# Moving the row tiles 2 to 4 of an output projection from their own stage into the last steps of a scan

## The chip, the cores and the metric

One core of a Trainium2 chip runs the whole program. The metric is device time in microseconds (us) for one execution, lower is better.

## The reference

One layer of a diffusion backbone over 2048 latent tokens of width 1024, with 256 context tokens. What matters here is the middle: a projection gives the inputs of three groups of heads (pooling, Mamba-2 SSD, gated DeltaNet), whose outputs stand beside each other as the 1024 columns of the mixer's output, and one output projection follows with a gated residual; then a router and a mixture of experts.

```python
s_lat, _, _ = ssd_stream(pl[1], pl[2], pl[3], *ssd_p, ssd_sf, ssd_sb)
g_lat, _, _ = gdn_stream(to_column_major(pl[4]), ...)          # a scan over chunks of 64, both directions
lat = jnp.concatenate([pool_branch(pl[0], pool_w, pool_scale), s_lat, g_lat], axis=-1) @ w_out
...
x = x + m_lat[2][:, None] * mix_lat
h_lat = modulate(rms_norm(x, norm2_g[l]), m_lat[3], m_lat[4])
x = x + m_lat[5][:, None] * expert_choice_ffn(h_lat, router_w[l], ...)
```

Of the 1024 rows of `w_out` (8 row tiles of 128) the tiles 0 and 1 meet the pooling's columns, 2 to 4 the SSD's and 5 to 7 the DeltaNet's.

## The kernel before, in words

The program has four stages: the input projection (to some 760 us), the scan (some 800 to 1523 us), the output stage (projection, norm and router, to 1713 us) and the mixture of experts.

**The scan** is recorded step by step from a list `plan`: `at(when, f)` puts a piece of work at a place `when`, counted in steps, and the pieces are recorded sorted by it. There are 36 chunk steps of the DeltaNet (`NSTEP`); preparing a chunk (`gdn_prep`, `gdn_inv`) runs ten steps (`LAG`) ahead of the chain `gdn_chain(n)`, which carries the state from chunk to chunk and so stands at the places n + 9.9 to n + 10.7. The SSD (`ssd_f`) stands at the places 9 to 28. From place 36 on only the chain and its last merges are left: the drain. TensorE's instructions keep the recorded order while the scan is recorded (`TE.order`, which ties each to the one before); on the other engines, and after the scan on TensorE too, a scheduler orders them.

A step of the chain: `pv<-kv` and `pv<-gS,w` (matmuls into the bank `pv`), ACT copies `vn` out of it; `po<-gS,qg` and `po<-vn,xqr` make the output in the bank `po`, of which there is one; `pc<-vn,ke` and DVE's `gS` make the next state. In its second half a step also adds the other direction (`po<-oe,turned`), and `gdn_out` scales the result out of `po` (ACT `osq`, a few small DVE operations, DVE `oe`) and stores it (`go_d<-oe`). The `pm` matmuls belong to `gdn_w` and to the merges of the triangular inverse.

**The fills.** The mixer's outputs of pooling and SSD lie in `mix_d`, transposed, before the DeltaNet is done. A fill multiplies some row tiles of one token tile t (16 of them) into one column half c (2 of 512), adds a partial sum and stores it: in `x0_d`, from which the output stage goes on. `sums[c][t]` holds how many row tiles are done and where the sum lies. `fill` is a generator in three pieces: the loads (`mx` from `mix_d`, `x`, which is the tile `fx`), the split of `mx` in a high and a low part (ACT and DVE), and the multiplication, `mm3` per row tile (three matmuls, high by high, high by low, low by high), with the DVE add and the store. Before the change the fills do row tiles 0 and 1 (`K0 = 2`), one per step: the first column half at the places 4 to 19, the second at 20 to 35, six matmuls each, in the bank `po`. The tile `fx` has three buffers, the `mx` tile (`fm`) and its parts (`fmh`, `fml`) two.

**The output stage.** `prep(t)` loads the row tiles that are left (`mx`), the chain's output `go` (four DMAs) and the partial sums `xo`; it splits row tiles 2 to 4, transposes `go` on TensorE, multiplies it into the last three row tiles (the gate) and splits them. `project(t)` multiplies the row tiles from `sums[h][t][0]` to 8 for both halves. `router(t)` transposes the new rows, multiplies them by the router's weights and writes the normed rows `h2`.

The weights of row tiles 2 to 4 are loaded by `load_1` (first half, place 36.5) and `ssd_end` (second half, place 28.5, when the SSD's tiles come free).

## Time and profile before

| | us |
|---|---|
| median of 3 timed runs | 2447.54 (2445.14 to 2454.45) |
| the profiled execution | 2454.28 |
| its span in the trace | 2452.5 |
| TensorE busy | 2119.1 (86%) |
| DVE, ACT, POOL busy | 1512.6, 1010.9, 771.3 |
| mean granted TensorE clock | 0.914 |

The busy time of an engine is an average over stages that have different limits, and a matmul's listed duration overlaps the next one's. So the stretches around the change are read one by one. PE is TensorE's multiplications, PEld its weight loads, DVE is VectorE, ACT ScalarE, POOL GpSimd, SP SyncE. A clock of 1.00 is 2.4 GHz all the time, 0.50 would be 1.2 GHz all the time.

### The profile page before, as it was taken

The page shows a single profiled execution, that of the slowest core. Times are in us where ns is not written, and L with a number is a line of the kernel's source. Part 1 is how long each engine was busy: PE and PEld are TensorE (multiplying, and loading weights), DVE is VectorE, ACT ScalarE, POOL GpSimd, SP SyncE. Part 2 cuts the span into 40 slices and gives each one's busy share as a digit, 9 for nine tenths or more (in the row PEclk, how much of TensorE's full clock was granted, in tenths as well). Part 3 has the DMA queues.
Part 4 walks back from the last instruction along what each step waited for, and adds up shares of the span by engine and source line. Part 5 has one row for each costly group of instructions (what it writes and reads, how often), then busy time and mean ns, then how long its engine had stood idle before and what let it go on. Part 6 is the DMA issues. An engine that isn't in the chain of part 4 may idle for free. (4 is left out here: it accounts for less than half of the span.)

```text
span 2452.5 us, 55979 instructions
## 1 busy us (share of the span) xinstructions
PE 2119.1 (86%) x22825; PEld 1816.0 (74%) x22825; DVE 1512.6 (62%) x3357; ACT 1010.9 (41%) x1916; POOL 771.3 (31%) x712
## 2 busy tenths in 40 slices
PE   4789999989987688989878788999199999988886
PEld 2788888878865467768766676787199999987785
DVE  6766776756755544545535443544757667689876
ACT  5443334544324235434443222454144444455552
POOL 1002332354421524434422122344331111124453
PEclk8899999999988779989998778999599999999998
DMA  7442345665435956666655432754447787778883
GB/s 233 117 110 91 82 124 145 168 172 126 128 86 143 277 146 167 166 175 184 186 163 154 138 94 73 244 197 139 171 156 212 233 227 223 231 256 282 303 283 138
DMA packets 323452, 425.77 MB, mean 174 GB/s; under 512 B 48875, under 2 KB 214650, under 8 KB 322170
## 3 DMA queue, kind: packets, MB, share of 16 engines
q1 hardware_dynamic: 294266, 356.07, 48.8%
q0 software_dynamic: 14816, 50.03, 7.7%
q10 hardware_dynamic: 14112, 16.10, 1.9%
q8 instruction: 179, 2.93, 0.5%
q14 instruction: 79, 0.65, 0.1%
HBM read 302.80 MB, written 126.71 MB: 175 GB/s over the span
## 5 line engine op out<-in xcount | busy, mean ns | idle before, releaser
L90 PE MATMUL pj<-hTh,wh 128*128 128x512 f32 (+1 forms) x800 | 308.6, 386 | 4.7 <-ACT wh L221 3.8
L90 PE MATMUL pj<-hTl,wh 128*128 128x512 f32 (+1 forms) x800 | 309.0, 386 | 0.0
L90 PE MATMUL pj<-hTh,wl 128*128 128x512 f32 (+1 forms) x800 | 307.8, 385 | 0.9 <-DVE wl L222 0.9
L491 DVE SCALAR_TENSOR_TENSOR acc<-u,PV,acc 128x512 f32<-128x512 f32 (+1 forms) x320 | 273.1, 900 | 55.0 <-ACT acc L489 36.4
L1727 ACT ACTIVATE wh<-wr 128x1024 fp32r<-128x1024 f32 x192 | 202.3, 1056 | 252.5 <-PE pgate L90 74.6
L1729 DVE TENSOR_TENSOR wl<-wr,wh 128x1024 fp32r<-128x1024 f32 x176 | 223.7, 1276 | 102.4 <-ACT wh L1727 102.2
L90 PEld LDWEIGHTS pj<-hTh,wh 128*128 128x128 f32 x800 | 154.2, 193 | 36.8 <-ACT wh L221 4.1
L90 PEld LDWEIGHTS pj<-hTh,wl 128*128 128x128 f32 x800 | 153.6, 192 | 31.7 <-DVE wl L222 1.6
L90 PEld LDWEIGHTS pj<-hTl,wh 128*128 128x128 f32 x800 | 154.0, 192 | 30.2 <-issue 0.7
L90 PE MATMUL pgate<-xel,wh 128*128 128x256 f32 x512 | 150.6, 294 | 2.9 <-DVE xel L222 2.9
L90 PE MATMUL pgate<-xeh,wh 128*128 128x256 f32 x512 | 148.7, 290 | 3.8 <-ACT xeh L221 3.7
L90 PE MATMUL pgate<-xeh,wl 128*128 128x256 f32 x512 | 150.1, 293 | 0.0
L90 PE MATMUL pup<-xeh,wh 128*128 128x256 f32 x512 | 149.1, 291 | 0.0
L90 PE MATMUL pup<-xel,wh 128*128 128x256 f32 x512 | 147.5, 288 | 0.0
L90 PE MATMUL pup<-xeh,wl 128*128 128x256 f32 x512 | 147.5, 288 | 0.0
L542 POOL TENSOR_TENSOR aw<-aw,sc 128x1024 f32<-128x1024 f32 x32 | 66.1, 2065 | 256.5 <-DMA aw<-in_ada_w_dram 252.0
L1826 POOL DMA_INDIRECT x_d<-ye,idx x30 | 48.8, 1626 | 203.2 <-DVE ye L1820 128.6
L90 PE MATMUL pdown<-wh,hh 128*128 128x512 f32 x256 | 103.3, 403 | 7.4 <-DVE ye L1820 3.0
L1128 ACT ACTIVATE Db<-xk 32x192 f32<-32x192 f32 (+2 forms) x160 | 55.1, 344 | 126.1 <-DVE xk L1111 124.6
L90 PEld LDWEIGHTS pgate<-xeh,wh 128*128 128x128 f32 x512 | 101.1, 198 | 5.1 <-ACT xeh L221 4.8
L90 PEld LDWEIGHTS pgate<-xel,wh 128*128 128x128 f32 x512 | 101.1, 198 | 3.1 <-DVE xel L222 3.1
L90 PE MATMUL pdown<-wh,hl 128*128 128x512 f32 x256 | 100.6, 394 | 0.6 <-DVE hl L222 0.6
(562 smaller groups left out, 5520.6 us busy)
## 6 DMA issues: line engine op xcount, KB each, us to landing
wr<-in_exp_w_gate_dram SPq DMA_DIRECT2D x64, 512.0 KB
wr<-in_exp_w_up_dram SPq DMA_DIRECT2D x64, 512.0 KB
wr<-in_exp_w_down_dram SPq DMA_DIRECT2D x64, 512.0 KB
aw<-in_ada_w_dram SPq DMA_DIRECT2D x32, 512.0 KB
kq<-qk_d SPq DMA_DIRECT2D x36, 384.0 KB
xb<-xb_d SPq DMA_DIRECT2D x35, 320.0 KB
wr<-in_w_in_dram SPq DMA_DIRECT2D x21, 512.0 KB
aw<-in_ada_w_dram SPq DMA_DIRECT2D x8, 1024.0 KB
```

Of the source, the lines that this page charges most:

```text
L90: return self.pin(nc.tensor.matmul(*args, **kw))
L491: V.scalar_tensor_tensor(av, u[:, s0 - 2 + i:s0 - 2 + i + w], cw[:, i, cb:cb + 1], av, op0=OP.mult, op1=OP.add)
L542: G.tensor_tensor(w, w, sc2[:, :, 0:1].to_broadcast([P, KT, P]), op=OP.mult)
L1128: S.activation(D_b[b][QS[q], sl:sl + w, :], xk[QS[q], h0:h0 + w, c:c + 32], AF.Copy)
L1727: S.activation(wh, w, AF.Copy)
L1729: (G if nw[0] <= 16 else V).tensor_tensor(wl, w, wh.bitcast(F32), op=OP.subtract)
L1826: G.indirect_dma_start(out=x2_d, out_offset=rows_of(e, h), in_=ys[h], in_offset=None, compute_op=OP.bypass if late else OP.add)
```

## The change

The fills are of three kinds now. `fill_0` is as before, for the first column half alone (places 4 to 19). `fill_1` takes the second column half, row tiles 0 to 4 in one go (15 matmuls), at the places 31 to 45.25, 0.95 apart. `fill_2` takes the first half again, row tiles 2 to 4 (9 matmuls), from `x0_d` to the new `x1_d`, at the places 38.4 to 45.9, half a step apart. Both use the ring `pp` of three banks in place of `po`, and tiles `fk`, `fkh`, `fkl` (two buffers each) in the room that the SSD leaves. `load_0(1)` moves from place 20 to `ssd_end`. Since `prep` and `project` go by `sums`, the output stage has row tiles 5 to 7 left, 18 matmuls per token tile where there were 36.

```diff
--- before.py
+++ after.py
@@ -185,6 +185,7 @@
     mrow_d = dram("mrow_d", [4, D])
     mcol_d = dram("mcol_d", [P, 16])
     x0_d = dram("x0_d", [T, D])
+    x1_d = dram("x1_d", [T, D])
     x2_d = dram("x2_d", [T, D])
     h2_d = dram("h2_d", [T, D])
 
@@ -1297,7 +1298,7 @@
             V.tensor_tensor(wl, w, wh.bitcast(F32), op=OP.subtract)
         wo[c].update(rows)
 
-    def fill(c, t, k1, dst, tiles):
+    def fill(c, t, k1, dst, tiles, ring):
 
         k0, src = sums[c][t]
         sums[c][t] = k1, dst
@@ -1309,19 +1310,36 @@
         yield
         split(mh, ml, mx)
         yield
-        po = bank(pb, "po", [512], 1)
+        po = bank(pb, ring, [512], NPP if ring == "pp" else 1)
         for k in range(n):
             mm3(po, mh[:, k, :], ml[:, k, :], *wo[c][k0 + k], k == 0, k == n - 1)
         V.tensor_tensor(x, po, x, op=OP.add)
         SY.dma_start(dap(dst, t * P * D + 512 * c, [[D, P], [1, 512]]), x)
 
-    def fill_0(c, t):
-        if t == 0:
+    def late_tiles(n):
+        return [wps[0].tile([P, KA, P], F32R if q else F32, name="fk" + q, bufs=2)[:, 0:n] for q in ("", "h", "l")]
+
+    def load_0(c):
+        if True:
             wh, wl = (p0.tile([P, K0, 512], F32R, name="f" + q) for q in "hl")
             load_wout(c, {k: (wh[:, k, :], wl[:, k, :]) for k in range(K0)},
                       (p0.tile([P, 512], F32, name="fx", bufs=3) for _ in range(3)))
-        return fill(c, t, K0, x0_d, lambda n: [p0.tile([P, K0, P], F32R if q else F32, name="fm" + q, bufs=2)
-                                               for q in ("", "h", "l")])
+
+    def fill_0(t):
+        if t == 0:
+            load_0(0)
+        return fill(0, t, K0, x0_d, lambda n: [p0.tile([P, K0, P], F32R if q else F32, name="fm" + q, bufs=2)
+                                               for q in ("", "h", "l")], "po")
+
+    def fill_1(t):
+
+        return fill(1, t, KA, x0_d, late_tiles, "pp")
+
+    def fill_2(t):
+
+        return fill(0, t, KA, x1_d, late_tiles, "pp")
+
+    wps = []
 
     def rows_3(tiles):
         return {K0 + k: tuple(t[:, k * 512:(k + 1) * 512] for t in tiles) for k in range(KA - K0)}
@@ -1377,15 +1395,22 @@
     for t in range(18):
         j = SSD0 + t
         along(ssd_f(t), *(j + q for q in (-0.4, 0.12, 0.26, 0.46, 0.56, 0.64, 0.74, 1.05, 1.9)))
-    for i, (c, t) in enumerate((c, t) for c in range(2) for t in range(NT)):
-        gen = []
-        at(FILL0 + i - 0.9, lambda c=c, t=t, gen=gen: gen.append(fill_0(c, t)) or next(gen[0]))
-        for q in (-0.3, 0.04):
-            at(FILL0 + i + q, lambda gen=gen: next(gen[0], None))
+    def fills(f, place):
+        for t in range(NT):
+            gen = []
+            at(place(t) - 0.9, lambda t=t, gen=gen: gen.append(f(t)) or next(gen[0]))
+            for q in (-0.3, 0.04):
+                at(place(t) + q, lambda gen=gen: next(gen[0], None))
+
+    fills(fill_0, lambda t: FILL0 + t)
+    fills(fill_1, lambda t: SSD0 + 22 + 0.95 * t)
+    fills(fill_2, lambda t: NSTEP + 2.4 + 0.5 * t)
 
     def ssd_end():
         stS.close()
         wp = stS.enter_context(tc.tile_pool(name="wout", bufs=1, reuse_waits="tile"))
+        wps.append(wp)
+        load_0(1)
         load_wout(1, rows_3([wp.tile([P, (KA - K0) * 512], F32R, name="wo" + q) for q in "hl"]),
                   (wp.tile([P, 512], F32, name="wr", bufs=4) for _ in range(4)))
 
```

What this does to TensorE's order, at one step of the drain. Before, from the output matmuls of a chain step to the state's part of the next one (`pm<-y` and `pm<-Yt` are the merge's and `gdn_w`'s; each row stands for all that follow each other, so x12 is a row of small matmuls):

```order
L90 MATMUL po<-vn,xqr 64x64 x12
L90 MATMUL po<-oe_16610,turned 128x384
L90 MATMUL pm<-y_16763,A_6362 64x32 x12
L90 MATMUL pv<-kv,Yt_6368 64x64 x12
L90 MATMUL pm<-Yt_6369,kw 64x64 x12
L90 MATMUL pv<-gS,w 64x64 x12
```

And in the changed kernel:

```order
L90 MATMUL po<-vn,xqr 64x64 x12
L90 MATMUL po<-oe_16679,turned 128x384
L90 MATMUL pm<-y_16854,A_6363 64x32 x12
L90 MATMUL pv<-kv,Yt_6369 64x64 x12
L90 MATMUL pm<-Yt_6370,kw 64x64 x12
L90 MATMUL pp<-kq,fkh 128x512 x2
L90 MATMUL pp<-kq,fkl 128x512
L90 MATMUL pp<-kq,fkh 128x512 x2
L90 MATMUL pp<-kq,fkl 128x512
L90 MATMUL pp<-kq,fkh 128x512 x2
L90 MATMUL pp<-kq,fkl 128x512
L90 MATMUL pv<-gS,w 64x64 x12
```

Nine 128x512 matmuls of a `fill_2` (weights in `kq`, the tile that `load_1` fills) stand now between `pm<-Yt,kw` and `pv<-gS,w`.

A little earlier in the same step, before, from the end of a merge's multiplications on:

```order
L90 MATMUL pm<-A_6360,Yd 32x32 x24
L90 MATMUL pc<-vn,ke 64x64 x12
L90 MATMUL pm<-y_16763,xk 64x32 x12
L90 MATMUL po<-vn,xqr 64x64 x12
L90 MATMUL po<-oe_16610,turned 128x384
```

In the changed kernel:

```order
L90 MATMUL pm<-A_6361,Yd 32x32 x24
L90 MATMUL pp<-kq,fkh 128x512 x2
L90 MATMUL pp<-kq,fkl 128x512
L90 MATMUL pp<-kq,fkh 128x512 x2
L90 MATMUL pp<-kq,fkl 128x512
L90 MATMUL pp<-kq,fkh 128x512 x2
L90 MATMUL pp<-kq,fkl 128x512
L90 MATMUL pc<-vn,ke 64x64 x12
L90 MATMUL pp<-fh,fkh 128x512
L90 MATMUL pp<-fl,fkh 128x512
L90 MATMUL pp<-fh,fkl 128x512
L90 MATMUL pp<-fh,fkh 128x512
```

A second `fill_2` stands before `pc<-vn,ke`, and a `fill_1` behind it, of which four of its fifteen matmuls are shown (weights in `fh`, `fl` and then `woh`, `wol`). So a step of the drain has 33 such matmuls.

SyncE's queue in one step of the drain, before (the chain's loads and its two stores `go_d`):

```order
L1067 DMA xqr<-xq_d 128x384
L1071 DMA oe_17051<-oe_d 128x384
L1279 DMA go_d<-oe 64x384 x2
L1060 DMA kv<-kv_d 64x768
L1061 DMA kv<-kvr_d 64x768
```

In the changed kernel, from the stores `go_d` to the next step's `oe`:

```order
L1280 DMA go_d<-oe 64x384 x2
L1317 DMA x_d<-fx 128x512
L1307 DMA fk<-mix_d 128x384
L1309 DMA fx<-x_d 128x512
L1317 DMA x_d<-fx 128x512
L1307 DMA fk<-mix_d 128x640
L1309 DMA fx<-x_d 128x512
L1317 DMA x_d<-fx 128x512
L1307 DMA fk<-mix_d 128x384
L1068 DMA xqr<-xq_d 128x384
L1309 DMA fx<-in_x_dram 128x512
L1072 DMA oe_17252<-oe_d 128x384
```

Three fills' stores (`x_d<-fx`; both `x0_d` and `x1_d` are shown as `x_d`), `fk` loads and `fx` loads stand between the chain's DMAs, each `fx` load two or three places behind a store.

## Rows read from the trace of the kernel before

**Rows 1.** Busy time by stretch (engines in the order PE, PEld, DVE, ACT, POOL, each with its instructions), then the granted TensorE clock as a share of full speed, the share of the DMA engines, GB/s. The cuts are the starts of the chain's `vn` at steps 10, 21, 28 and 35, then the first late multiplication of the output projection.

```profile
1106.90:1318.76 211.86, 181.68 (x4267) 153.44 (x4269) 103.56 (x262) 92.00 (x272) 79.62 (x92) 0.94 0.61 174
1318.76:1438.55 119.79, 95.66 (x2480) 80.45 (x2483) 56.35 (x135) 36.92 (x103) 23.76 (x25) 0.79 0.45 129
1438.55:1519.16 80.61, 66.55 (x1958) 57.87 (x1955) 27.20 (x66) 22.12 (x58) 19.53 (x24) 0.81 0.35 95
1519.16:1536.65 17.49, 9.49 (x81) 7.36 (x81) 6.91 (x21) 1.91 (x6) 3.83 (x66) 0.91 0.28 72
1536.65:1713.00 176.35, 173.78 (x1027) 142.67 (x1027) 87.21 (x272) 85.95 (x220) 72.15 (x30) 0.99 0.59 197
```

**Rows 2.** The same columns by single steps of the drain, from one `vn` to the next.

```profile
1438.55:1454.37 15.82, 12.73 (x351) 10.97 (x352) 6.04 (x14) 3.25 (x10) 5.06 (x7) 0.68 0.41 114
1454.37:1464.32 9.95, 8.91 (x351) 7.84 (x351) 2.84 (x6) 3.24 (x10) 1.42 (x2) 1.00 0.53 144
1464.32:1481.96 17.64, 14.54 (x346) 12.56 (x346) 5.41 (x13) 3.24 (x9) 5.41 (x7) 0.62 0.24 64
1481.96:1491.34 9.38, 9.09 (x351) 7.99 (x355) 2.69 (x9) 3.25 (x10) 2.22 (x3) 0.99 0.36 98
1491.34:1505.47 14.13, 9.81 (x338) 8.55 (x334) 5.60 (x13) 6.07 (x13) 2.67 (x4) 0.90 0.39 112
1505.47:1513.30 7.83, 6.76 (x146) 6.01 (x146) 2.52 (x9) 1.78 (x7) 1.62 (x2) 0.74 0.29 77
1513.30:1519.16 5.86, 4.70 (x122) 3.95 (x122) 2.10 (x6) 1.30 (x4) 1.13 (x2) 1.00 0.16 36
```

**Rows 3.** Waits of TensorE: who waited for whom, us in total, times, the longest. The first two rows are of 1438.6 to 1523 us, the last two of 1319 to 1438.6.

```profile
PE po L90 <- DVE oe L1277: 10.2, 5, 3.1
PE pm L90 <- ACT A L1198: 2.3, 1, 2.3
...
PE pm L90 <- ACT y L1191: 6.0, 1, 6.0
PE pm L90 <- ACT Yt L1204: 5.0, 1, 5.0
```

**Rows 4.** Single instructions in order of time (start, duration in us): the first and the tenth of ten 128x512 matmuls that follow each other, and the DVE add that empties a fill's bank.

```profile
1524.91 0.40 PE L90 MATMUL po<-kq,ml 128*128 128x512 f32 x1
...
1526.96 0.39 PE L90 MATMUL po<-woh,ml 128*128 128x512 f32 x1
...
1382.77 0.69 DVE L1315 TENSOR_TENSOR fx<-po,fx 128x512 f32<-128x512 f32 x1 [1.75 <-PE po L90]
```

**Rows 5.** SyncE's queue, single DMA issues in order of time (start, duration of the issue in us). First two fills of the scan (`x_d<-fx` is the store, `fm` and `fx` the loads of a later fill) with `qg` and `eg` between, then the chain's issues in the drain.

```profile
1281.89 0.33 SPq L1316 DMA_DIRECT2D x_d<-fx  x1
1282.31 0.39 SPq L1306 DMA_DIRECT2D fm<-mix_d  x1
1284.21 0.33 SPq L1308 DMA_DIRECT2D fx<-in_x_dram  x1
1284.64 1.34 SPq L1051 DMA_DIRECT2D qg<-qk_d  x2
1290.95 1.08 SPq L1053 DMA_DIRECT2D eg<-gx_d  x2
...
1300.28 0.33 SPq L1316 DMA_DIRECT2D x_d<-fx  x1
...
1304.31 0.33 SPq L1308 DMA_DIRECT2D fx<-in_x_dram  x1
...
1487.41 0.33 SPq L1067 DMA_DIRECT2D xqr<-xq_d  x1
...
1488.26 0.33 SPq L1071 DMA_DIRECT2D oe<-oe_d  x1
...
1491.50 1.27 SPq L1279 DMA_DIRECT2D go_d<-oe  x2
...
1492.88 0.64 SPq L1060 DMA_DIRECT2D kv<-kv_d  x1
```

**Rows 6.** The output stage: busy time in 120 us of it (columns as in rows 1), the add of the projection with its first and last start, and four groups of instructions in these 120 us (count, busy us, mean ns).

```profile
1560.00:1680.00 120.00, 120.00 (x707) 98.69 (x706) 60.29 (x193) 62.30 (x158) 53.43 (x23) 1.00 0.61 206
...
L1523 DVE TENSOR_TENSOR xo<-po,xo x32: 680/692/692, 1544.6 to 1706.4; 128x512 f32<-128x512 f32 x32
...
L1557 POOL TENSOR_TENSOR h<-h,mrow 128x1024 f32<-128x1024 f32 x12 | 28.8, 2402 | 67.6 <-ACT h L1556 67.6
L1558 POOL TENSOR_TENSOR h<-h,mrow 128x1024 f32<-128x1024 f32 x11 | 26.5, 2410 | 0.9
L222 DVE TENSOR_TENSOR ml<-mx,mh 128x384 fp32r<-128x384 f32 x23 | 15.0, 652 | 0.3 <-ACT mh L221 0.3
L221 ACT ACTIVATE mh<-mx 128x384 fp32r<-128x384 f32 x23 | 12.1, 525 | 37.1 <-PE po L90 29.2 <-DVE mx L1477 7.9
```

**Rows 7.** TensorE around the end of the chain: the first and the last of the output projection's early matmuls, and the transposes of the first `go` tile with the wait ahead of them.

```profile
1522.77 0.91 PE L90 MATMUL po<-kq,mh 128*128 128x512 f32 x2
...
1529.00 0.39 PE L90 MATMUL po<-kq,ml 128*128 128x512 f32 x1
...
1534.58 0.87 PE L93 MATMUL ptr<-ident,go 128*128 128x128 f32 x3 [5.19 <-DMA go<-go_d]
```

**Rows 8.** Busy time of 40 us at the start of the scan, columns as in rows 1.

```profile
800.00:840.00 40.00, 20.96 (x143) 16.41 (x141) 20.52 (x55) 9.23 (x25) 19.32 (x22) 0.74 0.99 263
```

## The prediction

> **What bounds the kernel now.** I read four views in this order: the busy time by stretch, the same by single steps of the drain, the waits of TensorE, and single rows of a fill and of the SyncE queue.
>
> Cutting the span where the chain's `vn` starts gives five stretches [rows 1]: steps 10 to 21 of the program (1106.90 to 1318.76 us), steps 21 to 28 (to 1438.55), the drain, steps 28 to 35 (to 1519.16; here steps are the chain's number n, ten behind the plan's), the tail up to the first late multiplication of the output projection (to 1536.65), and the output stage (to 1713.00). The reader is to see two kinds of stretch. In the output stage TensorE is busy 173.78 of 176.35 us at a granted clock of 0.99, and DVE, ACT and POOL have half of their time free: TensorE bounds it. In the drain TensorE is busy 66.55 of 80.61 us at 0.81, so part of the time is idle, and part runs at 1.2 GHz.
>
> By single steps [rows 2] the drain splits further. Each of the first five steps has some 350 TensorE instructions. In the steps at a clock of 0.99 and 1.00 these take 9.38 and 9.95 us; in the steps at 0.68 and 0.62 they take 15.82 and 17.64 us, with 12.73 and 14.54 us busy instead of about 9. The waits [rows 3] show what idle time there is: of the drain, 10.2 us before `po<-gS,qg`, for DVE's `oe` of the step before (five times), and 2.3 us for ACT's `A`; of the stretch before it, 6.0 and 5.0 us behind ACT's `y` and `Yt`.
>
> **The unit.** A 128x512 matmul that follows another one starts 0.228 us after it at full clock (nine from 1524.91 to 1526.96 [rows 4]); its listed duration is latency and is not used. The change moves such matmuls and neither adds nor removes any: 192 in fills and 576 in the output stage before, 480 and 288 after. Counted in the order of TensorE between the same `vn`: 57 leave the steps up to the 21st (six of them just before 1106.90 us); steps 21 to 28 go from 24 to 105; the drain from 0 to 231; after the last `vn` there are 33; the output stage loses 288.
>
> **Steps 10 to 21.** 57 x 0.228 = 13.0 us of TensorE work goes. TensorE is busy for 181.68 of 211.86 us there [rows 1], so I take that share of it, 11 us. Bounds: 13 us, and 5 us if most of these fills stood ahead of a wait.
>
> **Steps 21 to 28.** 81 matmuls more are 18.5 us. The stretch has 24.1 us of TensorE idle [rows 1], but 11.0 of it are the two waits behind `y` and `Yt` [rows 3], which stop TensorE in its pinned order, so nothing behind them can fill them. The other 13 can be covered: 18.5 - 13 = 5.5, say 6 us longer. Bounds: 18.5 (nothing covered) and -5 (the idle time covered, and some of the work at 0.79 now at full clock).
>
> **The drain.** I take the steps at their full-clock pace: five of 9.67 us (the mean of 9.38 and 9.95), then 7.83 and 5.86 as they are, 62.0 us; the 231 matmuls add 52.7; the waits for `oe` in the last two steps, some 2 us each by the mean of 10.2 over five [rows 3], are covered, since nine matmuls (2.1 us) now stand between `pm<-Yt,kw` and `pv<-gS,w`. That gives 111 us for 80.6, 31 longer. Why full clock: in the rows the clock is 0.99 to 1.00 in the steps that are nearly without waits (9.09 us busy of 9.38) and in the output stage, and 0.62 and 0.68 in the steps where TensorE stood 2 to 3 us for `oe`; with 33 matmuls in each step the waits for `oe`, `w` and `y` have other work in front of them. The Trainium skill, "TensorE: Matmul & The Clock Gate", section "What's actually happening", says the same as a rule: throttled is the default state and activity releases it. By the rule the drain is at 2.4 GHz and costs these 31 us; by the drain's own row (0.81) the same matmuls would take 231 x 0.228 / 0.81 = 65 us, less 14 of idle, 51 us, and the whole sum would be no gain. Bounds without it: 53 us (nothing covered), and 52.7 - 14.1 (idle) - 9.3 (what the two slow steps are busy beyond 9 us each) = 29.
>
> What each fill brings besides: an ACT split (0.5 to 0.7 us by the 128x384 row, 0.525 [rows 6]), a DVE split and a DVE add (0.65 and 0.69 [rows 4, 6]), three per step, 4 us more on DVE and 2 on ACT. DVE is busy 27.20 of 80.61 us and ACT 22.12 [rows 1], so both hide; if that cover is gone, each lands on the chain. The weight rows 0 and 1 of the second column half are loaded later by some eight steps; costed at nothing, since that is well before the first new fill.
>
> **The tail.** 24 matmuls (5.5 us) come before the last `po`, of which about 2 us cover a wait: 3.5 us. Nine more stand in the hole where TensorE waits for the `go` tile (5.19 us of wait, and 27 matmuls of tiles 0 and 1 which the kernel before does there, from 1522.77 to 1529.00 [rows 7]): nothing. Bounds 0 and 5.5.
>
> **The output stage.** Of its 576 matmuls 27 are done in that hole, 549 after it. 288 remain, and since each needs the gated row tiles, none of them fits into the hole. So TensorE's work goes from 173.8 to 173.8 - 261 x 0.228 = 114 us, 7.1 us for each of 16 tiles. What is late next: POOL has 2 x 2.4 us per tile, ACT 62.30 us in 120 us, DVE 60.29 [rows 6], that is 4.8 to 5.4 us per tile of 10.4 us (first to last `xo`, 1544.6 to 1706.4, 31 intervals of half a tile). All fit under 7.1 us, but not by much; where TensorE idled for 2.6 us I allow 12, which gives 126 us, 50 shorter. Bounds: 60 shorter (as gapless as now), and 16 shorter if the DMA engines stay at their share of 0.61: a tile moves 2112 KB now (`mx` 384, `go` 192, `xo`, `x2` and `h2` 512 each) and 1920 after, so 176 x 0.91 = 160. I stay near the first since the DMA share reached 0.99 elsewhere [rows 8].
>
> **Sum.** -11 + 6 + 31 + 3.5 - 50 = -20.5 us. The profiled execution took 2454.3 us, 6.7 above the median of the three timed runs, 2447.5; taken from the median, 2427 us. The ends of the bounds add up to -49 and +56.
>
> **Rivals.**
> *The SyncE queue sets the drain's pace (slower).* It issues in order, and the load of a fill's `fx` waits until the store of an older `fx` has landed, because there are three buffers: from store to the end of that load 2.65 us in one place and 4.36 in another [rows 5]. Three fills per step are 8.0 to 13.1 us; the chain's own issues (`xqr`, `oe`, two `go_d`, two `kv`, half of `qg` and `eg`) are 4.4. So 12.4 to 17.5 us per step against TensorE's 9.5 + 33 x 0.228 = 17.0. At the upper end SyncE is level with TensorE, and while it waits for a store, the chain's loads stand behind. It decides above 17.0 + 20.5/7 = 19.9 us per step; above 21.7 the kernel is measurably slower. At 22 us: 2462. Against it: loads for the chain are issued a whole step ahead, and TensorE paces the stores. The Trainium skill's page "DMA: Bandwidth & Descriptors", "Anatomy of one DMA", puts about 2.0 us of fixed time on each transfer, mostly for the write's receipt; with that instead of the rows the queue would need 12 us per step and would not bind. The two rows (2.3 and 4.0 us from store to load) say that it is sometimes twice that.
> *The output stage doesn't follow TensorE, or the drain stays at its clock (no change).* The stage comes down by 30 instead of 50, or the drain grows by 51: between -1 and 0, 2447.
> *More is hidden.* Both stretches at their lower bound, the stage at -60: 2402.
>
> **How the numbers follow.** A difference of 0.5% (12 us) is about what a measurement of this kernel can tell from none. Forecast, 12 to 35 us shorter: 0.45. More hidden: 0.12. No change: 0.25. Slower: 0.18. So faster 0.57, same 0.25, slower 0.18. The range leaves out the far end of the SyncE rival and of the last one: 2402 to 2460; that of the forecast alone is 2412 to 2435.
>
> **What would show it.** In the profile after: the drain (28th to 35th `vn`) 105 to 125 us long, at a clock over 0.9, with the wait for `oe` mostly gone; the output stage 120 to 135 us with TensorE over nine tenths busy; steps 10 to 21 some 202 us. It is wrong if the drain is over 130 us with TensorE waiting for `fkh`, `fkl` or `xqr` (SyncE), or if the stage stays above 145 us with TensorE waiting for `mh`.

## The result, and the profile after

The changed kernel takes 2467.2 us (median of 5 runs, 2459.6 to 2471.9), 1.0077 times the kernel before with a 95% interval of 1.0051 to 1.0102: slower by 0.8%, where 2427 us had been forecast. The profiled execution took 2466.5 us, with a span of 2464.7.

Busy time by stretch in the changed kernel, with the columns of [rows 1] and the same cuts: `vn` 0, 10, 21, 28 and 35 of the chain, the first late multiplication of the output projection, the last one, and the first count of the expert search (`pc<-cnt`, with which the mixture of experts begins), up to which the two kernels differ.

```profile
887.81:1094.04 206.23, 183.67 (x3954) 154.22 (x3951) 107.47 (x261) 88.33 (x267) 88.57 (x106) 0.91 0.59 164
1094.04:1306.89 212.85, 182.56 (x4216) 154.42 (x4218) 93.75 (x247) 88.91 (x263) 79.31 (x92) 0.86 0.51 142
1306.89:1435.78 128.89, 112.46 (x2579) 94.10 (x2581) 64.72 (x143) 41.17 (x107) 26.36 (x28) 0.84 0.52 150
1435.78:1555.92 120.14, 116.14 (x2182) 94.00 (x2170) 49.50 (x113) 35.24 (x81) 19.60 (x22) 0.96 0.64 195
1555.92:1577.70 21.78, 11.37 (x87) 8.28 (x87) 7.89 (x21) 2.44 (x6) 3.82 (x66) 0.80 0.44 136
1577.70:1705.45 127.75, 112.81 (x693) 93.11 (x694) 100.94 (x220) 63.87 (x181) 59.22 (x25) 0.94 0.69 231
1705.45:1732.86 27.41, 10.93 (x77) 8.43 (x76) 19.57 (x51) 9.69 (x29) 17.79 (x9) 0.62 0.33 115
```

Some of the kernels run later share the scan of one of the two, so a stretch can be read more than once. The table has the first pair of profiles, then means: for the stretches of the scan of three profiles with the old scan and five with the changed one, for the output stage of two with the old stage and the one above.

| stretch, us | before | after | difference | difference of the means | forecast |
|---|---|---|---|---|---|
| steps 0 to 10 | 215.0 | 206.2 | -8.8 | -2.1 | 0 |
| steps 10 to 21 | 211.9 | 212.9 | +1.0 | +0.1 | -11 |
| steps 21 to 28 | 119.8 | 128.9 | +9.1 | +9.5 | +6 |
| drain | 80.6 | 120.1 | +39.5 | +41.9 | +31 |
| tail to the first late multiplication | 17.5 | 21.8 | +4.3 | +4.3 | +3.5 |
| output stage, to the first count | 182.7 | 155.2 | -27.5 | -29.3 | -50 |

Three rows carry the miss: the output stage gave back 21 to 22 us less than forecast, the steps ahead of the drain gave none of their 11, and the drain took 9 to 11 us more. The means add up to +24 us, where the medians of the timed runs are 20 apart. (The stretch before step 0 and the mixture of experts, which the change doesn't touch, make the spans' difference of 12.2 us in the first pair complete with -4.0 and -1.3.)

In the output stage TensorE is no longer the bound: 112.8 of 127.8 us to the last multiplication, 8.0 us per token tile where [rows 1] had 173.8 of 176.4. DVE is busy for 100.9 us of these 127.8, instead of half of the time. Two groups of DVE's small operations account for that: `oss`, which adds the two halves' sums of squares, and `AFF`, which writes the router's result. The first two rows are of the output stage before, the other two of the stage after (count, busy us, mean ns, idle before).

```profile
L1554 DVE TENSOR_SCALAR AFF<-sme,mxv 128x16 f32<-128x16 f32 x16 | 5.4, 335 | 0.1
L1535 DVE TENSOR_TENSOR oss<-oss 128x1 f32<-128x1 f32 x16 | 3.5, 221 | 0.0
```

```profile
L1579 DVE TENSOR_SCALAR AFF<-sme,mxv 128x16 f32<-128x16 f32 x16 | 23.2, 1453 | 0.5
L1560 DVE TENSOR_TENSOR oss<-oss 128x1 f32<-128x1 f32 x16 | 20.6, 1285 | 8.3 <-ACT sq L1549 8.3
```

Thirty-two operations on 1 or 16 columns took 8.9 us and take 43.8. Single instructions of the stage after (start, duration) show what they stand behind:

```profile
1657.74 2.40 POOL L1582 TENSOR_TENSOR h<-h,mrow 128x1024 f32<-128x1024 f32 x1 [3.71 <-ACT h L1581]
1660.21 2.34 POOL L1583 TENSOR_TENSOR h<-h,mrow 128x1024 f32<-128x1024 f32 x1
...
1667.32 2.40 POOL L1582 TENSOR_TENSOR h<-h,mrow 128x1024 f32<-128x1024 f32 x1 [4.76 <-ACT h L1581]
```

```profile
1658.31 1.84 DVE L1560 TENSOR_TENSOR oss<-oss 128x1 f32<-128x1 f32 x1 [1.23 <-ACT sq L1549]
...
1660.45 2.14 DVE L1579 TENSOR_SCALAR AFF<-sme,mxv 128x16 f32<-128x16 f32 x1
...
1667.76 0.69 DVE L223 TENSOR_TENSOR x2l<-ptr,x2h 128x512 fp32r<-128x512 f32 x1 [1.10 <-ACT x2h L222]
```

`oss` ends at 1660.15, POOL's first operation on `h` at 1660.14; `AFF` ends at 1662.59, POOL's second at 1662.55. This is no single case: 25 of these 32 operations took over 0.4 us, and all 25 end within 0.1 us of a POOL operation's end; in the kernel before it was two of 32. `x2l`, which reads one operand from the PSUM bank `ptr`, takes its 0.69 us in the middle of a POOL operation. The Trainium skill's page "SBUF — State Buffer", section "SBUF: two separate sides", states the rule: DVE and GpSimd share a port pair, and the pair is "an exclusive lock, not a bandwidth split", which DVE needs for its two-port modes and, against a GpSimd operation that reads SBUF, for two operands in SBUF; whichever starts first keeps it until its instruction is over. These rows agree with it. Behind the two stand `mx` and the splits, and TensorE waits for those (waits of TensorE from 1556 to 1725: us in total, times, longest; a row of 12.3 us for the load of `go` stands above them, 9.2 of it ahead of the stage):

```profile
PE ptr L93 <- DVE mx L1502: 9.1, 4, 2.3
PE pr L90 <- DVE x2l L223: 4.4, 4, 1.8
PE ptr L93 <- DVE x2l L223: 2.5, 1, 2.5
```

The end of the stage, from the last multiplication to the first count, doubled as well, from 13.3 to 27.4 us: the last tiles' small operations meet POOL again (one `ory` of 2.13 us), and the search's first tile waits for the store of an `h` that lies in its room.

```profile
1731.03 0.42 DVE L1624 COPY vh<-pt 128x256 uint16<-128x256 uint16 x1 [5.08 <-DMA h_d<-h]
```

The drain went nearly as forecast. By single steps (first, second and fifth; columns of [rows 2]), and the waits of TensorE in all of it, against 10.2 us for `oe` in [rows 3]:

```profile
1435.78:1455.89 20.11, 18.51 (x376) 14.81 (x367) 7.50 (x20) 5.13 (x14) 3.36 (x5) 0.92 0.73 208
1455.89:1472.96 17.07, 17.07 (x384) 13.81 (x384) 6.94 (x16) 5.13 (x13) 4.54 (x4) 1.00 0.66 196
...
1507.19:1529.71 22.52, 20.12 (x379) 16.70 (x378) 9.64 (x21) 7.97 (x16) 3.18 (x3) 0.85 0.57 178
```

```profile
PE pm L90 <- ACT A L1199: 2.1, 1, 2.1
PE po L90 <- DVE oe L1278: 1.6, 1, 1.6
```

Three of the five long steps take 17.0 to 17.2 us with TensorE never idle at a granted clock of 1.00, which is the forecast's 9.67 + 33 x 0.228 = 17.2. The fifth has the wait for `A`, and its clock is 0.85.

In steps 10 to 21 a wait is new, at the matmuls `pp<-xb,sE`; the kernel before has no row for `sE` there.

```profile
PE pp L90 <- ACT sE L946: 11.5, 7, 3.4
```

TensorE's clock is lower there too: 0.86 to 0.89 in the five profiles of the changed scan, 0.91 to 0.94 in the three of the old one. So 51 matmuls less in these steps, 11.6 us at full clock, took only 2 us off TensorE's busy time (181.9 us on average for 184.0), and its idle time grew by as much.

### The profile page after: what moved, and what is told of

Read it like the earlier page. It is cut to its first block, busy times and chain, and to the rows that moved or that the text cites. A ratio compares the mean times of both kernels' runs of the same rounds, so it can differ in the third digit from the quotient of the medians.

```text
span 2464.7 us, 56134 instructions
## 1 busy us (share of the span) xinstructions
PE 2125.8 (86%) x22825; PEld 1815.3 (74%) x22825; DVE 1556.5 (63%) x3373; ACT 1010.4 (41%) x1916; POOL 771.3 (31%) x712
## 5 line engine op out<-in xcount | busy, mean ns | idle before, releaser
L492 DVE SCALAR_TENSOR_TENSOR acc<-u,PV,acc 128x512 f32<-128x512 f32 (+1 forms) x320 | 272.7, 899 | 53.6 <-ACT acc L490 34.9
L1129 ACT ACTIVATE Db<-xk 32x192 f32<-32x192 f32 (+2 forms) x160 | 55.1, 344 | 114.3 <-DVE xk L1112 112.2
L90 PE MATMUL pdown<-wl,hh 128*128 128x512 f32 x256 | 101.8, 398 | 0.0
```

What stands on the lines that cost most here:

```text
L90: return self.pin(nc.tensor.matmul(*args, **kw))
L492: V.scalar_tensor_tensor(av, u[:, s0 - 2 + i:s0 - 2 + i + w], cw[:, i, cb:cb + 1], av, op0=OP.mult, op1=OP.add)
L1129: S.activation(D_b[b][QS[q], sl:sl + w, :], xk[QS[q], h0:h0 + w, c:c + 32], AF.Copy)
```

## The experiments

Ratios are to the kernel before, run beside each, with 95% intervals.

### How far a stretch moves by itself

> The kernel before, profiled a second time, to see how far the stretches of the scan move by themselves. In the first pair of profiles the steps up to the 10th vn were 8.8 us shorter after the change (206.2 for 215.1) and steps 10 to 21 were 1.0 longer (212.9 for 211.9), where the prediction had 0 and -11. If the change is the cause, this run repeats 215 and 212 within some 3 us. If it is the executions' own spread, these two stretches move by 5 to 10 us here. The drain (80.6) and the output stage (first late multiplication to the first count of the expert search: 182.7) should repeat within 2 us by either theory.

Measured: 213.7, 213.0, 118.6 us for the three stretches of the scan, an output stage of 186.2 us, 3.5 longer than in the first profile, and a drain of 74.4 at a clock of 0.89, 6.2 shorter:

```profile
1435.58:1509.97 74.39, 62.19 (x1958) 54.19 (x1955) 27.78 (x66) 22.31 (x58) 19.39 (x24) 0.89 0.38 103
```

So a drain with waits spreads (the steps of 15.8 and 17.6 us in [rows 2] took 13.6 and 12.7 here), and one pair of profiles prices it to some 6 us only. Steps 0 to 10 came to 206 to 216 us in five profiles of the changed scan: the -8.8 of the first pair was spread for the most part.

### The output stage: DVE and POOL

**POOL's operations left out.**

```diff
-            G.tensor_tensor(h2, h2, A2, op=OP.mult)
-            G.tensor_tensor(h2, h2, B2, op=OP.add)
```

> The changed kernel without POOL's two operations on h2 (it leaves out the multiplication by A2 and the addition of B2). Theory: in the output stage small DVE operations (AFF, oss) end exactly when POOL's operation on h ends, 1.3 to 1.5 us instead of 0.2 to 0.3, because DVE and POOL exclude each other; with DVE free only 4 to 5 us per token tile are left to it, and TensorE's 7.1 us per tile bound the stage. Expected by it: AFF at 0.25 us and oss at 0.15 us, first to last late multiplication 114 to 120 us (128 in the changed kernel), TensorE over 95% busy there, the whole stage to the first count of the search 128 to 138 (155), the kernel 18 to 27 us faster than the changed one, about 2443. Rival, latency: the two buffers of mx and the order of the work set 8 us per tile; then first to last stays 126 to 130 and only the end of the stage gets shorter, by up to 8 us: about 2459. Rival, DMA: the stage has a DMA share of 0.77 to 0.80 at its start; then the same 126 to 130.

Measured: 2439.8 us, ratio 0.9952 (0.9928 to 0.9976), 27 us under the changed kernel. The stage, to the last multiplication and to the first count, then the two groups:

```profile
1584.62:1696.78 112.16, 108.00 (x692) 90.64 (x693) 72.12 (x229) 66.09 (x185) 0.00 (x0) 0.95 0.82 273
1696.78:1708.57 11.79, 7.71 (x76) 6.17 (x75) 8.48 (x41) 8.64 (x25) 0.88 (x1) 0.86 0.58 207
```

```profile
L1579 DVE TENSOR_SCALAR AFF<-sme,mxv 128x16 f32<-128x16 f32 x16 | 3.7, 233 | 0.5
L1560 DVE TENSOR_TENSOR oss<-oss 128x1 f32<-128x1 f32 x16 | 2.5, 158 | 4.5 <-ACT sq L1549 4.5
```

7.0 us per tile: the forecast's pace for TensorE (7.1), with the DMA share higher (0.82) than in the changed kernel (0.69). Both rivals fall. Of the 31 us that POOL's operations cost the stage, half lie ahead of the last multiplication and half behind it (127.8 and 27.4 us for 112.2 and 11.8).

**The same two operations on DVE** (`V.` for `G.` in the two lines).

> The changed kernel with the two operations on h2 on DVE in place of POOL; no work is left out. DVE gets two 128x1024 operations per tile, some 2.4 us by the one such row of the stage (1.23 us each). Theory (DVE and POOL exclude each other): DVE's own work per tile is 97.2 us in 127, less 2.4 us per tile of standing behind POOL, that is 3.8 us, plus 2.4: 6.2 us under TensorE's 7.1; no small operation over 0.4 us, first to last late multiplication 115 to 122 us, the kernel 2443 to 2455, that is even with the kernel before or a little faster. Rival, latency or DMA: 128 us or more stay, since DVE gets more work: 2462 to 2475.

Measured: 2453.1 us, 0.9999 (0.9977 to 1.0020). 113.3 us to the last multiplication, an end of 20.7: with the whole work done the stage takes 133.9 us, 49 less than in the first profile before and 51 less than in the mean of two, the forecast's number, and the kernel is even.

```profile
1587.13:1700.40 113.27, 109.39 (x698) 90.62 (x698) 92.86 (x244) 65.14 (x180) 0.00 (x0) 0.95 0.78 261
1700.40:1721.06 20.66, 7.91 (x71) 6.59 (x70) 17.18 (x59) 10.16 (x31) 0.88 (x1) 0.68 0.48 168
```

**The two long DVE operations on ACT.**

```diff
-            V.tensor_tensor(ss[:, 0:1], ss[:, 0:1], ss[:, 1:2], op=OP.add)
-            V.tensor_scalar(ss[:, 0:1], ss[:, 0:1], 1.0 / D, EPS, op0=OP.mult, op1=OP.add)
+            S.activation(ss[:, 0:1], ss[:, 0:1], AF.Identity, bias=ss[:, 1:2])
+            S.activation(ss[:, 0:1], ss[:, 0:1], AF.Copy, bias=EPS)
-            V.tensor_scalar(AFF[:, t % 2, t // 2, :], e, mxv[:, 2:3], None, op0=OP.mult)
+            S.activation(AFF[:, t % 2, t // 2, :], e, AF.Copy, scale=mxv[:, 2:3])
```

(and `scale=1.0 / 32` in the `Square` that fills `ss`)

> The changed kernel with the two small DVE operations that are longest in the stage moved to ACT (AFF, and the sum of oss with its scale and constant); POOL keeps h2; no work is left out. Theory: the 23.2 + 20.6 us of these 32 operations, 34.9 of it standing behind POOL, leave DVE. ACT gets 0.6 us per tile on 4. What is late next: the four small operations of the inverse root (ort, ory) and the splits may meet POOL in their place. So 117 to 124 us from first to last late multiplication, the kernel 2450 to 2458. If the stall only moves to the next DVE operation with two operands in SBUF: 126 to 130 us and 2462 to 2468; the rows of ort, ory and ml then show it. Rivals, latency or DMA: 126 to 130 as well, but with no long DVE operation left.

Measured: 2459.5 us, 1.0034 (1.0009 to 1.0060); 118.2 us to the last multiplication, an end of 26. More than half of the stall found the next operations with two operands in SBUF, two steps of the inverse root that take 0.15 us each without POOL's operations; 20 of the 34.9 us are here now:

```profile
L130 DVE TENSOR_TENSOR ort<-ory 128x1 f32<-128x1 f32 x16 | 17.1, 1066 | 0.4 <-ACT ory L149 0.3
L131 DVE TENSOR_TENSOR ort<-ort,oss 128x1 f32<-128x1 f32 x16 | 9.1, 569 | 0.1
```

**DVE for tiles 0 to 13, POOL for the last two** (`eng = V if t < 14 else G`).

> The changed kernel with h2's two operations on DVE for the token tiles 0 to 13 and on POOL for the last two. Nothing is left out. In after_dve the end of the stage, from the last multiplication to the first count of the search, took 20.7 us, since four operations of 1.2 us stand on DVE ahead of the last AFF; in the kernel before, with POOL, it took 13.3, without these operations 11.8. Expected: 112 to 114 us from first to last late multiplication, an end of 13 to 16, 5 to 7 us less than after_dve; ratio to the kernel before 0.996 to 1.000. If the last two tiles meet DVE on POOL's port as in the changed kernel (27 us): 1.000 to 1.004.

Measured: 2453.4 us, 0.9999 (0.9982 to 1.0017). 113.0 us to the last multiplication, but an end of 24.1: POOL at the end is no better than DVE.

**The control: DVE in the kernel before.**

> The control: the kernel before with h2's two operations on DVE in place of POOL. By the theory TensorE bounds its output stage (173.8 of 176.4 us busy) and DVE waits 4.4 us per half tile for po, so no small operation meets POOL, and only the end after the last multiplication can change by 1 to 3 us: ratio 0.998 to 1.001. If POOL's collisions had cost the kernel before as well, its output stage gets shorter by 5 us or more: ratio 0.996 or less.

Measured: 1.0037 (1.0013 to 1.0061), slower than expected. Its profiled execution doesn't show where: the scan (213.1, 117.9, 74.9) and the time from the last `vn` to the first count (200.8 us, 200.2 and 203.7 in two profiles of before) are not longer. But it was the fastest of the twelve (2451.4 us for a median of 2457.2). What the runs lose stays open; a gain by this edit alone is excluded.

### The steps ahead of the drain

**Row tiles 0 and 1 of the second half stay early**, only 2 to 4 are late: `fill_1` does `K0` row tiles in the bank `po` as before, with their weights loaded at the old place, and a new `fill_3` is `fill(1, t, KA, x1_d, late_tiles, "pp")`.

```diff
-    fills(fill_1, lambda t: SSD0 + 22 + 0.95 * t)
+    fills(fill_1, lambda t: FILL0 + 16 + t)
+    fills(fill_3, lambda t: SSD0 + 22 + 0.95 * t)
```

> The changed kernel, but row tiles 0 and 1 of the second column half stay where they were before the change (six matmuls per step at the places 20 to 35, bank po); only row tiles 2 to 4 of both halves are multiplied late (9 matmuls each, at the same late places). Nothing is left out. Theory: before the change the six matmuls of a fill stood right ahead of pp<-xb,sE, which waits for ACT's sE; taken away, TensorE waits there itself (11.5, 11.1, 12.5 and 11.6 us in seven or eight waits in the four profiles with the change, none listed before), so they were free where they stood and 57 x 0.228 = 13 us of TensorE work came off steps 10 to 21 for nothing. Put back, steps 10 to 21 stay at 211 to 215 us and the wait for sE goes, while the drain has some 39 matmuls less (nine for fifteen in about 6.5 tiles) and steps 21 to 28 some 18 less: 9 and 4 us. So 12 to 14 us faster than the changed kernel, ratio to the kernel before 0.996 to 1.001, with the output stage as in the changed kernel (155 us). Rival: the fills cost their 13 us there and the difference is the executions' spread; then steps 10 to 21 take 222 to 226 us and the kernel is as the changed one, ratio 1.003 to 1.008.

Measured: 2476.1 us, 1.0109 (1.0067 to 1.0151): slower still. Steps 10 to 21, 21 to 28, and the drain:

```profile
1105.55:1324.11 218.56, 191.87 (x4276) 162.41 (x4278) 103.74 (x264) 93.00 (x274) 79.83 (x92) 0.90 0.60 169
1324.11:1453.39 129.28, 106.25 (x2543) 88.43 (x2547) 65.53 (x152) 40.70 (x110) 21.68 (x25) 0.85 0.56 163
1453.39:1568.08 114.69, 106.73 (x2148) 86.01 (x2145) 48.03 (x109) 33.45 (x80) 21.09 (x24) 0.96 0.65 197
```

The wait for `sE` is gone, but steps 10 to 21 are 6 us longer than in the changed kernel, neither the theory's 0 nor the rival's 13, and the ratio is outside both; steps 21 to 28 and the drain didn't shorten as their matmuls did. Steps 10 to 21 are 6 us longer than in the kernel before as well, which has the same early fills (218.6 and 217.4 us again in keep_early_dve and keep_half): the late work costs that much there, of which its nine new matmuls are 2 us.

> As keep_early, and h2's two operations on DVE in place of POOL. Nothing is left out. By the theory the two gains add: the output stage 134 us as in after_dve, the scan as in keep_early. Expected ratio to the kernel before 0.991 to 0.996, about 2438 us: faster than both kernels. If the fills cost their 13 us where they stood: ratio 0.999 to 1.002.

Measured: 1.0035 (1.0009 to 1.0061); steps 10 to 21 again 218.6, the stage 112.0 + 20.6. The stage's gain repeats; no gain of the scan shows.

**The second half's fills left out of the kernel before** (`range(1)` for `range(2)` in the loop over `c`, and `sums[1] = [(K0, a["x"])] * NT`).

> The kernel before without the sixteen fills of the second column half (it leaves out row tiles 0 and 1 of that half: loads, splits, 96 matmuls, adds and stores, and the loading of their weights). In steps 10 to 21 of the program this removes what the change removes there, and adds nothing anywhere. Theory: the six matmuls of a fill stood ahead of pp<-xb,sE, which waits for ACT's sE, and were free there: steps 10 to 21 stay at 210 to 215 us (211.9, 213.0, 213.1 in three profiles with the fills) and TensorE waits for sE for 10 to 13 us there. Rival: the fills cost their 13 us, and what keeps the changed kernel at 213 us is its new loads and weights: then 198 to 203 us here.

Measured: 2420.0 us in its one run. Steps 0 to 10, 10 to 21, 21 to 28, the drain, and the wait of TensorE in steps 10 to 21:

```profile
892.66:1092.06 199.40, 181.62 (x3954) 152.77 (x3952) 105.56 (x261) 87.37 (x266) 88.49 (x106) 0.92 0.59 161
1092.06:1298.25 206.19, 172.99 (x4199) 146.43 (x4201) 90.44 (x237) 87.63 (x262) 79.36 (x92) 0.90 0.50 142
1298.25:1404.66 106.41, 85.35 (x2491) 73.76 (x2491) 54.63 (x133) 36.03 (x100) 25.23 (x27) 0.81 0.47 130
1404.66:1481.21 76.55, 62.71 (x1910) 54.80 (x1910) 26.34 (x66) 21.90 (x59) 18.30 (x23) 0.87 0.36 100
```

```profile
PE pp L90 <- ACT sE L945: 10.3, 8, 2.7
```

Steps 10 to 21 lose 68 instructions of TensorE, some 15 us, and get 6.5 us shorter than the mean before, again neither 0 nor 13. TensorE's busy time falls by 11 us, and its idle time, with the new waits for `sE`, grows by 4.5. With keep_early's 6 us from the other side, a fill there costs a little under half of its matmuls. That is as good as single profiles allow: the two with late_weights' scan (below) have 213.9 and 219.2 us for these steps. Steps 0 to 10 lose 14 us by the means, 7 to 11 of it in step 8, which loads the fills' weights (17.5 us for 24.8 to 28.4).

**The load of these weights.** The change records `load_0(1)` eight steps later. DVE's row for it, in the kernel before and in the changed one, both in step 8:

```profile
1059.85 0.75 DVE L1295 SCALAR_TENSOR_TENSOR fx<-fx,wscale 128x512 f32<-128x512 f32 x1 [7.37 <-DMA fx<-in_w_out_dram]
```

```profile
1053.11 0.75 DVE L1296 SCALAR_TENSOR_TENSOR fx<-fx,wscale 128x512 f32<-128x512 f32 x1 [7.49 <-DMA fx<-in_w_out_dram]
```

Only TensorE is pinned to the recorded order; the scheduler left this load where it was, and DVE stands 7 us for it. Reading it into a tile that comes free with the SSD's moves it:

```diff
-        load_0(1)
+        load_0(1, (wp.tile([P, 512], F32, name="wr", bufs=4) for _ in range(3)))
```

> The changed kernel, with the raw weights of load_0(1) read into the tile wr of the pool that opens when the SSD's tiles come free, in place of the tile fx. Nothing is left out. In the changed kernel load_0(1) is recorded eight steps later than before, but DVE's fx<-fx,wscale still runs in the 9th step (8 counted from nought), where DVE stands 7.4 to 7.6 us for the load fx<-in_w_out with the operations of the scan behind it; that step takes 25 to 27 us in the profiles before and after the change and 17.5 in before_nofill, which has no such load. Theory: this stall sets the step, and the recorded place alone had not moved it. Expected: that step 17 to 19 us, steps 0 to 10 some 7 us shorter (199 to 206 us), the load's rows behind the SSD instead, with 0 to 3 us more in steps 18 to 22: 4 to 8 us in all, ratio to the kernel before 1.004 to 1.006 in place of 1.0077. Rival: before_nofill's short step came from the fill that it leaves out, not from the load; then the step stays at 24 to 27 us.

Measured: 2468.8 us, 1.0073 (1.0048 to 1.0097), no different from the changed kernel. Step 8 fell to 18.4 us as expected and steps 0 to 10 to 198.8, but steps 18 and 20 took 25.5 and 23.8 (24.0 and 20.6) and steps 21 to 28 131.5. What the profile gains on balance is within the spread of the time.

> As late_weights, with h2 on DVE for the token tiles 0 to 13 as in after_mix. Nothing is left out. If the two gains add: ratio to the kernel before 0.996 to 0.998, the fastest of the kernels that do the whole work; if the weights' stall only moves to a later step: 0.999 to 1.001.

Measured: 0.9994 (0.9975 to 1.0013), as after_mix.

### How much to move

**The second half alone** (no `fills(fill_2, ...)`).

> One part of the change alone: the second column half in one go (fifteen matmuls) in the last steps, no second round for the first half, whose row tiles 2 to 4 stay in the output stage (27 matmuls per token tile there in place of 18). Nothing is left out. Drain: 126 matmuls less than the changed kernel, 28.7 us at full clock: 90 to 92 us (118.6 in the mean of four profiles). Output stage: 27 x 0.228 = 6.2 us and some 2.3 for the rest of a tile, 8.5 us per tile, above the 8.0 that DVE and POOL set in the changed kernel: TensorE bounds it again, 136 us and an end of 13 to 20, in all 150 to 155. So drain +13, steps 21 to 28 +10, stage -30 to -34 against the kernel before: 2440 to 2450, ratio 0.996 to 1.000. Rival: with half the fills the drain keeps its waits and its low clock (100 us or more) and the kernel is even: 2452 to 2458.

Measured: 2461.9 us, 1.0056 (1.0028 to 1.0084). The drain, the stage (here from the first token tile's row tile 2 on) and its end:

```profile
1438.22:1536.37 98.15, 86.98 (x2064) 72.42 (x2062) 33.49 (x78) 27.07 (x64) 18.73 (x22) 0.93 0.44 133
...
1546.46:1699.58 153.12, 146.90 (x857) 119.35 (x858) 106.59 (x260) 77.63 (x207) 71.72 (x65) 0.95 0.69 227
1699.58:1713.85 14.27, 6.47 (x59) 4.94 (x57) 11.48 (x33) 5.92 (x18) 8.93 (x5) 0.81 0.22 89
```

The rival's drain, near 100 us. The stage is TensorE's again, but it got only 23 us shorter (177.5 for 200.2, from the last `vn`), not 30, and the kernel is slower than either side expected.

**144 matmuls late** (keep_early without `fill_2`).

> The smallest form of the move: row tiles 0 and 1 of both halves as in the kernel before, and of the second half alone the row tiles 2 to 4 in the last steps (9 matmuls per token tile, 144 in all, for the change's 240 and 144). Nothing is left out. From the stretches measured so far: the drain gets 66 matmuls, 15 us, in place of 231; only_second's 105 made it 21.5 us longer, so 11 to 15 longer here; steps 21 to 28 6 to 10 longer; the output stage as in only_second, 20 to 24 shorter. Sum -7 to +5: ratio 0.997 to 1.002. If each late matmul costs the same wherever it stands (0.228 us in the drain, as much in the stage), it is even; if the waits of the drain cover the first ones for nothing, it is at the lower end.

Measured: 2447.3 us, 0.9982 (0.9957 to 1.0007): even. The drain was 84.0 us, but steps 10 to 28 took 349.2, 18 more than the means before.

**96 matmuls late, the output stage left alone** (`K0` for `KA` in `fill_1`, no `fill_2`, weights as in late_weights), at the change's places (late_two) and at places in the drain (late_two_drain, the + line).

```diff
-    fills(fill_1, lambda t: SSD0 + 22 + 0.95 * t)
+    fills(fill_1, lambda t: NSTEP + 0.62 * t)
```

> The part of the move that the profiles leave as a possible gain: only row tiles 0 and 1 of the second column half (96 matmuls) are moved, from the places 20 to 35 to the places 31 to 45.25, with their weights as in late_weights; row tiles 2 to 4 of both halves stay in the output stage as in the kernel before (36 matmuls per token tile). Nothing is left out. From before_nofill, which has the same scan without these 96 matmuls (steps 0 to 10 199.4 us, 10 to 21 206.2, 21 to 28 106.4, drain 76.5): the weights' load adds 2 to 7 us in steps 18 to 20, about 42 matmuls in steps 21 to 28 add 10, about 45 in the drain add 10 less what they cover of its 10 to 14 us of waits, 2 to 10. Output stage as before (200 us). Sum against the kernel before (means 213.4, 212.7, 118.8, 76.6): -14 -2 -2 +6, that is -8 to -16: ratio 0.994 to 0.997, faster than both kernels. Rival: where the fills stand makes no difference, and what before_nofill gained is the 96 matmuls themselves (22 us) and the 7 us of the load: then 0.999 to 1.002.

Measured: 2456.3 us, 1.0030 (1.0009 to 1.0051), a miss; 217.7, 120.7 and 87.0 us in steps 10 to 21, 21 to 28 and the drain of its profiled execution, the longest of the twelve.

> As late_two, with the sixteen fills at the places 36 to 45.3, 0.62 apart, so that steps 21 to 26 have none of them and the drain some 66 matmuls. Expected: steps 21 to 28 at 108 to 114 us, the drain 84 to 90; the sum within 4 us of late_two: ratio 0.994 to 0.998. If the drain's waits (10 us for oe before the change) are covered for nothing, it is the faster of the two.

Measured: 2437.8 us, 0.9961 (0.9938 to 0.9983): faster than both kernels. The same four stretches of the scan:

```profile
890.19:1089.62 199.43, 181.12 (x3954) 152.10 (x3951) 104.85 (x258) 87.47 (x265) 88.42 (x106) 0.93 0.61 165
1089.62:1303.01 213.39, 176.53 (x4201) 149.52 (x4201) 92.40 (x238) 88.63 (x263) 79.16 (x92) 0.87 0.50 139
1303.01:1411.97 108.96, 89.31 (x2480) 75.76 (x2484) 59.15 (x151) 37.70 (x105) 22.85 (x26) 0.84 0.52 147
1411.97:1499.28 87.31, 75.52 (x2024) 62.09 (x2021) 33.22 (x88) 26.50 (x68) 21.64 (x24) 0.94 0.56 165
```

The drain takes the fills for 11 us more than the mean before; steps 21 to 28 and 0 to 10 give 10 and 14. This kernel moves the load of the fills' weights too, which is most of the 14: the changed kernel without the load's move had 206 to 216 us there, with it (late_weights) 198.8. What of the gain is the load's and what the matmuls' was not separated. In late_two the same matmuls stand some steps earlier, and steps 21 to 28 are 12 us longer; there TensorE waits for ACT's `A`, `y` and `Yt` in its pinned order (9.6, 5.0 and 4.6 us in late_two) whatever else it has to do. That this is why the two kernels are 18 us apart is argued, not tested.

## Why the prediction was wrong, by its own steps

**The output stage (-50, measured -27.5) failed, and with it the sum.** The step was "All fit under 7.1 us, but not by much": it set each engine's busy time per tile against TensorE's pace, engine by engine. DVE's and POOL's times can't be laid side by side. In the kernel before, most of POOL's 4.8 us per tile fell into DVE's waits for `po`: 50 of its 72 us up to the last multiplication. At 8 us per tile these waits are gone (rows of DVE's waits for `po`, before and after: us in total, times, longest), and 34.9 us of standing came into DVE's queue.

```profile
DVE xo L1523 <- PE po L90: 75.3, 27, 4.5
```

```profile
DVE xo L1548 <- PE po L90: 1.4, 2, 1.2
```

The step had no term of its own for the end of the stage either, which grew by 14 us. TensorE's part of the step was right: 7.0 us per tile and -59 us without POOL's operations, -49 with them on DVE (-61 and -51 against the mean of two profiles before). The rival "the output stage doesn't follow TensorE" came true with its price (30 instead of 50), by a mechanism that it didn't name; the DMA share, which the lower bound rested on, was not the limit. The sign that the prediction gave for this miss, over 145 us with TensorE waiting for `mh`, came with another wait: 1.2 us for `mh`, 9.1 for `mx`.

**Steps 10 to 21 (-11, measured 0) failed.** The share of time in which TensorE is busy was taken as the share of a matmul that lies on the path. The fills' matmuls stood ahead of a wait for `sE`, which the step had only as its bound of 5 us. And it took the clock as unchanged, although the drain's step reckoned with it: with the fills gone, TensorE stands for `sE`, and its clock is 0.86 to 0.89 for 0.91 to 0.94, so that the work that is left takes longer. Of the some 6 us that were to be had (before_nofill, keep_early), 15 of the new matmuls, which fall into these steps, take 3.4. That the clock took the rest is argued from these rows; no run tested it alone.

**The weights' load ("loaded later by some eight steps; costed at nothing") was wrong in what it said, right in its cost.** The load didn't move. Moved for real in the changed kernel (late_weights), it brought no time that shows.

**Steps 21 to 28 (+6, measured +9.5)** lay inside the bounds of -5 to 18.5. **The tail (+3.5, measured +4.3)** was right.

**The drain (+31, measured +39.5; 41.9 by the means) was right in its mechanism:** the clock at 0.96, the wait for `oe` down from 10.2 to 1.6 us, steps of 17.1 us, 120.1 us inside the 105 to 125 given. Its size was off by 9 us. The terms add up to 110.7 us for the drain and 120.1 were measured: 2.9 and 5.3 us more in the two steps that kept waits, where the clock was 0.92 and 0.85, and 1.5 more in the last two. The profiled execution before also had the longest drain of three, 4 us over their mean, so that the real growth is a little larger still.

**The SyncE rival did not come.** The drain's waits have no row for `fkh`, `fkl` or `xqr`, and its step is 17 us, TensorE's. The kernel ended on that rival's side of the result for other reasons, and the range (2402 to 2460) missed by 7 us: nothing in it allowed for a stage at -30 and a larger drain together with nothing from the early steps. (What the prediction cites from the Trainium skill's page "DMA: Bandwidth & Descriptors", "Anatomy of one DMA", 2.0 us per transfer, is given there for transfers that GpSimd issues. SyncE issues these, and no run here separates that time.)

## What to carry to other kernels

When a change shortens the work of the engine that bounds a stage, ask not only whether the other engines fit into the new period, but which of them exclude each other: list DVE's operations whose operands lie in SBUF and POOL's, and look whether the old slack kept them apart. A removed operation is worth what stands right behind it in its queue: ahead of a wait it is worth less than its own time (here 6.5 us for 15), however busy the engine, and look whether the clock falls where it is gone. And work moved from one stretch that TensorE is busy in to another can gain the waits that it covers there and little else: of the moves tried, the one that paid was one of the two smallest, put wholly into the drain.

## What the runs showed of the hardware

A DVE addition of 128x1 takes 0.16 us on average in the run without POOL's operations, and took 1.84 behind one POOL operation on 128x1024 (2.40 us): the size of the small operation doesn't matter, the rest of the large one does. When the two longest were moved to ACT, the next one in line became nearly as long (1066 ns on average for `ort`). Not every DVE operation stands: in the stage after, 12 of the 16 reciprocals on 128x1 (`mxv`, one operand) and 10 of the 32 `x2l`, with one operand in PSUM, ran wholly inside a POOL operation at their usual 0.16 and 0.69 us.

TensorE's clock went both ways with the same move: in the drain, where matmuls came in, it rose from 0.81 to 0.96, and in steps 10 to 21, where matmuls left and a wait came, it fell from 0.94 to 0.86.
